# Moving the routing of each head group 13 dots ahead of its first fetch, pacing the linear attention by the fetches, and one more fetch buffer

## The chip, the cores and the metric

The kernel runs on one core of one Trainium2 chip. The metric is the device time in microseconds (us). The kernel before took 2400.81 us, the median of three runs that lie between 2400.66 and 2401.58 us.

## The reference, cut to what matters

256 tokens of width 1024 pass through three blocks: latent attention, gated linear attention and a convolution/attention mixer. The first two are each followed by a PEER layer, the third by a mixture of 32 experts. The change lies in the two PEER layers and in the linear attention between them. A PEER layer picks, for each token and each of 8 heads, 16 rows out of a table of 16384, and sums them with weights that depend on the rows:

```python
def peer_ffn(x, w_query, sub_keys, u_tab, v_tab):        # blocks of 128 tokens
    q = (xi @ w_query).reshape(B, T, 8, 2, 64)
    s = jnp.einsum('bthcd,cnd->bthcn', q, sub_keys)      # 2 x 128 scores per head
    s_top, i_top = lax.top_k(s, 16)
    cand = s_top[..., 0, :, None] + s_top[..., 1, None, :]
    best, pos = lax.top_k(cand.reshape(B, T, 8, 256), 16)
    idx = ...                                            # 16 rows of 16384 per head
    gate = jax.nn.softmax(best, axis=-1)
    h = gelu(jnp.einsum('bthkd,btd->bthk', u_tab[idx], xi))
    return jnp.einsum('bthk,bthkd->btd', gate * h, v_tab[idx])

def gla_mixer(x, ...):                                   # layer 1, between the PEER layers
    proj = x @ w_in                                      # 1024 x 3088
    log_a = log_sigmoid(g_low @ w_g2 + b_g) / 16
    o = chunked_gla(q, k, v, log_a)                      # 4 heads, a state carried over chunks of 64
    return (rms_norm(o) * silu(r)) @ w_o                 # 1024 x 1024
```

Every product is in float32, built from pairs of rounded parts where the code says `mm3`.

## The kernel before, in words

The stages follow each other: latent attention (`mla`), the two PEER layers with the linear attention woven in (`experts`, from some 150 us to 1620 us), the mixer and the mixture of experts. All that changes is in `experts`.

**Dots and fetches.** The tables u and v lie side by side in memory, so that one row has 2048 float32. A *fetch* (`meet`, L849) is an indirect DMA that GpSimd (POOL) issues: 128 tokens each get one row, into one buffer `g` of 128 x 2048. A ring of `NG` = 9 such buffers is used in turn. The *dot* that follows runs on VectorE (DVE, L129): the u half times the token `xs`, summed to `hs`. Two fetches make a pair (`NQ` = 2). After a pair, ScalarE (ACT) takes the Gelu of both sums (L858), DVE multiplies by the gates, ACT builds two diagonal matrices `dw` (L862), and TensorE (PE) adds diag(w) times the v half to the accumulators (L865). Only then is a buffer of the ring free for the fetch 9 further on. There are 2 layers x 2 token blocks x 8 heads x 16 rows = 512 fetches.

**Groups and routing.** The heads are taken in groups of two (in the very first block [0], [1], [2,3], [4,5], [6,7]; later [0,1], [2,3], [4,5], [6,7]). Group starts are therefore at fetch 0, 16, 32, 64, 96, 128 and so on by 32. *Routing* a group (`prepare` = `query`, then `route`) means the query product on PE, the scores, two rounds of top-16 on DVE, the row numbers `idx`, and the gates (`sm`, `gate`, with an exponential on ACT, L831). `prepare` is a Python generator; each `yield` ends one piece. While the dots of one group are written out, the pieces of the next group's routing are taken from the generator between them, `parts` = 7n+4 pieces (n heads) over the first 70% of the dots (`RT`); whatever is left runs after the group's last dot (`for _ in step: pass`). The code behind the last `yield`, which writes `idx` and the gates, runs only when the generator is asked once more than it has yields. It has 7n+4 yields in layer 0, block 0 (each head's query yields twice there), 5n+4 in layer 0, block 1, and 6n+4 in layer 1.

**Linear attention.** `gla` is a generator too, of 84 pieces for block 0 and 80 for block 1. Block 0 runs between the dots of layer 0, block 1 (fetches 128 to 255), block 1 between those of layer 1, block 0 (256 to 383); `BG` = 0.95 pieces per dot are asked for. Its carried state `S` has a tile of its own in the stage's pool.

**Order on the engines.** All DVE instructions of routing and dots are chained in the order in which they are written (`InOrder`); every engine runs its own queue in order, and a scheduler that simulates time decides where instructions of different threads stand in it. Weights come in by DMAs that SyncE (SP) issues, into four `raw` buffers.

Of the kernel before, what the change touches and what calls it, by code (L numbers as in the profile page):

```python
# [9 lines left out]
FT = mybir.dt.float32  # L10
# [109 lines left out]
class InOrder:  # L120

    def __init__(self, tc, engine):
        self.tc, self.engine, self.last = tc, engine, None
# [14 lines left out]
class K:  # L138
    def __init__(self, tc, ins, es):
        self.tc, self.nc, self.i = tc, tc.nc, ins  # L140
        nc = self.nc
        self.cp = es.enter_context(tc.tile_pool(name="cp", bufs=1))
        self.pp = es.enter_context(tc.tile_pool(name="pp", bufs=1))
        cp = self.cp
        self.h = self.pp.tile([128, 2, 1024], FT, name="h", tag="h")
        self.cols = cp.tile([128, NCOLS], FT, name="cols")
        self.iota = cp.tile([128, 128], FT, name="iota")
        nc.gpsimd.iota(self.iota, pattern=[[1, 128]], base=0, channel_multiplier=0,
                       allow_small_or_imprecise_dtypes=True)
        self.diag = cp.tile([128, 128], FT, name="diag")  # L150
        nc.gpsimd.iota(self.diag, pattern=[[1, 128]], base=0, channel_multiplier=-1,
                       allow_small_or_imprecise_dtypes=True)
        self.mhalf = cp.tile([128, 1], FT, name="mhalf")
        nc.gpsimd.memset(self.mhalf, -0.5)
        self.ident = cp.tile([128, 128], FT, name="ident")
        nc.vector.tensor_scalar(self.ident, self.diag, 0.0, None, op0=OP.is_equal)
        self.flip = 0
        self.ssq = {}
        self.psum = es.enter_context(tc.tile_pool(name="banks", bufs=1, space=PSUM, reuse_waits="tile"))
        self.ahead = []  # L160
        self.NQ, self.NG, self.RT, self.BG = 2, 9, 0.7, 0.95
        self.xb = {}
        self.MP, self.G1, self.G2, self.G3, self.G4, self.BK = 34, 0, 4, 2, 1, 3
        self.CP, self.QS, self.KS = 0, 1, 0
        self.gate = None
        self.junk = None
        self.WN, self.W0, self.WL = 5, 12, 4
        self.W1, self.W2 = 20, 13
        self.NRAW, self.NHL, self.NHL1 = 4, 12, 12
# [556 lines left out]
    def experts(self):  # L726
# [3 lines left out]
        with self.phase("peer", ps=(6, 7), pq=(2, 3)) as mp:  # L730
# [15 lines left out]
            def query(l, b, h):  # L746
                if (l, b, h) in qs:
                    return
                if l not in keys:
                    keys[l] = mp.tile([128, 256], FT, name="sk", bufs=2)  # L750
                    nc.sync.dma_start(keys[l], self.i[f"sk{l}"])
                it = its.setdefault((l, b), None) or self.units(self.i[f"pq{l}"])
                its[l, b] = it
                ws = [next(it), next(it)]
                for b in ((0, 1) if l == 0 else (b,)):
                    q = qs[l, b, h] = mp.tile([128, 128], FT, name=f"qT{b}", bufs=8 if b else 3)
                    xH, xL = self.xb[b]
                    p = self.ps("pq")
                    for c in range(8):
                        wH, wL = ws[c // 4]  # L760
                        s = slice((c % 4) * 128, (c % 4 + 1) * 128)
                        self.mm3(p[:, :128], wH[:, s], wL[:, s], xH[:, c, :], xL[:, c, :], c == 0, c == 7)
                    nc.scalar.activation(q, p[:, :128], AF.Copy)  # L763
                    yield
# [74 lines left out]
            def prepare(l, b, hs):  # L839
                for h in hs:  # L840
                    yield from query(l, b, h)
                yield from route(l, b, hs)

            def meet(l, b, idx, gate):
                hs = mp.tile([128, self.NQ], FT, name="hs", bufs=6)
                got = []
                for k in range(self.NQ):
                    g = mp.tile([128, 2, 1024], FT, name="g", bufs=self.NG)
                    nc.gpsimd.indirect_dma_start(out=g.rearrange("p a b -> p (a b)"), out_offset=None,  # L849
                                                 in_=self.i[f"puv{l}"],  # L850
                                                 in_offset=bass.IndirectOffsetOnAxis(ap=idx[:, k:k + 1], axis=0))
                    V.tensor_tensor_reduce(g[:, 0, :], g[:, 0, :], self.xs[b], 1.0, 0.0, op0=OP.mult,
                                           op1=OP.add, accum_out=hs[:, k:k + 1])
                    got.append(g)
                    if k < self.NQ - 1:
                        yield
                w = mp.tile([128, self.NQ], FT, name="w", bufs=6)
                nc.scalar.activation(w, hs, AF.Gelu)  # L858
                V.tensor_tensor(w, w, gate, op=OP.mult)
                for k, g in enumerate(got):  # L860
                    d = mp.tile([128, 128], FT, name="dw", bufs=5)
                    nc.scalar.activation(d, self.ident, AF.Copy, scale=w[:, k:k + 1])  # L862
                    left[l, b] -= 1
                    for n in range(2):
                        mm(y[b][n], d, g[:, 1, n * 512:(n + 1) * 512], start=False, stop=left[l, b] == 0,  # L865
                           skip_group_check=True)
                        if left[l, b] == 0:
                            self.square(b, n, y[b][n])
                yield

            def dots(batches):
                for t in batches:
                    yield from meet(*t)

            groups = []
            for l in range(2):
                for b in range(2):
                    left[l, b] = 128
                    first = [[0], [1]] if l == b == 0 else [[0, 1]]
                    groups += [(l, b, hs) for hs in first + [[2, 3], [4, 5], [6, 7]]]  # L880
            state = mp.tile([128, 4, 2, 256], FT, name="S")
            behind, pace, done = None, 0.0, 0
            for _ in prepare(*groups[0]):
                pass
            for i, (l, b, hs) in enumerate(groups):
                if l != b and hs[0] == 0:
                    behind, pace, done = self.gla(mp, 1 - b, state), 0.0, 0
                step = prepare(*groups[i + 1]) if i + 1 < len(groups) else iter(())
                n2 = len(groups[i + 1][2]) if i + 1 < len(groups) else 0
                parts = 7 * n2 + 4  # L890
                batches, ready = ready, []
                n = int(len(batches) * self.NQ * self.RT)
                taken = 0
                for k, _ in enumerate(dots(batches)):
                    while taken < parts and taken < (k + 1) * parts // n:
                        next(step, None)
                        taken += 1
                    if behind is not None:
                        pace += self.BG
                        while done < pace:  # L900
                            done += 1
                            if next(behind, 0) == 0:
                                behind = None
                                break
                if behind is not None and hs[-1] == 5:
                    for _ in behind:
                        done += 1
                    behind = None
                for _ in step:
                    pass  # L910
            nb = [mp.tile([128, 2, 1024], FT, name="g", bufs=self.NG).rearrange("p a b -> p (a b)")[:, :1024]
                  for _ in range(3)]
            self.load_gain(4, nb[2])
# [336 lines left out]
    def moe(self, out):  # L1250
        nc, tc = self.nc, self.tc
        y = self.y
        with self.phase("moe", ps=(2, 3, 6, 7)) as mp:
# [134 lines left out]
            def experts(once):  # L1388
                wts = weights(once)
                for q in range(8):  # L1390
# [58 lines left out]
                    for b in range(2):  # L1449
                        for n in range(2):  # L1450
                            mm(y[b][n], C[:, b, :], ys[:, n * 512:(n + 1) * 512], start=False, stop=False,
                               skip_group_check=True)

            experts(True)
            fin = self.pp.tile([128, 2, 1024], FT, name="fin", tag="h")
            sq1 = fin[:, 1, 512:640]
# [11 lines left out]
            with tc.For_i(1, rounds, 1):  # L1468
                nc.vector.tensor_scalar(rank, rank, -32.0, None, op0=OP.add)
                experts(False)  # L1470
# [39 lines left out]
```

## Time and profile before

| | before |
|---|---|
| median of the runs | 2400.81 us |
| the profiled execution, its own time | 2398.6 us |
| its span, first to last instruction | 2396.8 us |
| PE busy | 2040.0 us (85%) |
| DVE busy | 1414.2 us (59%) |
| ACT busy | 717.8 us (30%) |
| POOL busy | 618.2 us (26%) |
| mean DMA rate over the span | 355 GB/s |

The busy shares are means over stages with different limits. Within the PEER layers the useful row is the DMA rate in each slice of time: it has a level that it reaches again and again and never passes, and dips below it.

### The profile page before, as it was taken

Reading aid. Unit: us, or ns where it says so; the run is one execution under the profiler, and the core shown is the slowest. Engines: PE = TensorE matmul, PEld = TensorE weight load, DVE = VectorE, ACT = ScalarE, POOL = GpSimd, SP = SyncE. Lnnn points to the kernel's source line nnn. Section 1 sums busy time; section 2 is a strip of 40 time slices with the busy share of each in tenths; the row PEclk is TensorE's granted clock in tenths of the full one; section 3 lists DMA queues with packets and bytes.
Section 4 is the critical chain, followed back from the end, with each engine's and each line's share of the span. In section 5 each row is a group of like instructions: output and inputs, shape, how many; then the busy total and the mean of one; then the engine's idle time right before and its main releaser. Section 6 shows DMA issues by size and latency. Waiting matters only on the chain. (4 is left out here: it accounts for less than half of the span.)

```text
span 2396.8 us, 26752 instructions
## 1 busy us (share of the span) xinstructions
PE 2040.0 (85%) x8294; PEld 1078.1 (45%) x8296; DVE 1414.2 (59%) x3813; ACT 717.8 (30%) x1756; POOL 618.2 (26%) x665
## 2 busy tenths in 40 slices
PE   8998667678989778998887777779999989999997
PEld 7774223234445325654333332237899942222221
DVE  7767667668868667878766776657666640000001
ACT  6632211235343225544222221215545510000000
POOL 4123433443434442333444444320000000000000
PEclk9999999998999998999999999999999999999999
DMA  4369889999999998999999999984467699999996
GB/s 154 106 227 371 343 368 422 373 422 408 421 388 360 421 421 352 422 401 399 422 421 421 421 421 422 421 335 150 150 226 260 221 360 417 417 417 417 417 417 277
DMA packets 161780, 851.40 MB, mean 355 GB/s; under 512 B 18368, under 2 KB 19008, under 8 KB 96096
## 3 DMA queue, kind: packets, MB, share of 16 engines
q0 software_dynamic: 73728, 536.90, 54.4%
q1 hardware_dynamic: 87616, 312.20, 33.6%
q8 instruction: 69, 1.13, 0.2%
q14 instruction: 79, 0.65, 0.1%
q10 hardware_dynamic: 288, 0.52, 0.1%
HBM read 848.50 MB, written 1.05 MB: 354 GB/s over the span
## 5 line engine op out<-in xcount | busy, mean ns | idle before, releaser
L865 PE MATMUL ps<-g,dw 128*128 128x512 f32 x2048 | 973.8, 622 | 253.2 <-ACT dw L862 252.2
L849 POOL DMA_INDIRECT g<-in_puv_dram,idx x512 | 558.4, 1091 | 882.1 <-PE ps L865 482.6
L129 DVE CUSTOM_DVE_ANT_0 g<-g,xs 128x1024 f32<-128x1024 f32 x512 | 623.1, 1221 | 232.5 <-DMA g<-in_puv_dram,idx 221.3
L865 PEld LDWEIGHTS ps<-g,dw 128*128 128x128 f32 x2048 | 386.7, 197 | 787.8 <-issue 388.3
L262 DVE TENSOR_TENSOR wl<-raw,wh 128x512 fp32r<-128x512 f32 (+3 forms) x404 | 267.9, 678 | 118.9 <-ACT wh L260 107.7
L260 ACT ACTIVATE wh<-raw 128x512 fp32r<-128x512 f32 (+3 forms) x408 | 242.3, 614 | 150.8 <-PE ps L285 124.4
L858 ACT ACTIVATE w<-hs 128x2 f32<-128x2 f32 x256 | 51.9, 203 | 745.6 <-DVE hs L129 745.5
L1425 PE MATMUL ps<-we,xT 128*32 128x512 f32 x788 | 186.2, 600 | 21.2 <-DMA we<-in_e_gu_dram 21.2
L862 ACT ACTIVATE dw<-ident,w 128x128 f32<-128x128 f32 x512 | 177.4, 393 | 70.6 <-DVE w L129 66.4
L1430 DVE TENSOR_TENSOR hid<-hid,ps 128x512 f32<-128x512 f32 x8 | 5.5, 688 | 248.9 <-PE ps L1425 248.9
L284 PE MATMUL ps<-xH,wh 128*128 128x256 f32 (+1 forms) x456 | 130.3, 286 | 1.1 <-DVE sel L1117 1.1
L286 PE MATMUL ps<-xL,wh 128*128 128x256 f32 (+1 forms) x456 | 130.3, 286 | 0.0
L285 PE MATMUL ps<-xH,wl 128*128 128x256 f32 (+1 forms) x456 | 129.9, 285 | 0.0
L1425 PEld LDWEIGHTS ps<-we,xT 128*32 128x32 f32 x788 | 35.6, 108 | 162.9 <-DMA we<-in_e_gu_dram 119.0
L1459 POOL MEMSET fin<- 128x128 f32 x1 | 0.2, 204 | 405.5 <-PE ps L1425 405.5
L1443 PE MATMUL ps<-we,hT 128*32 128x512 f32 x400 | 96.4, 597 | 0.1
L284 PEld LDWEIGHTS ps<-xH,wh 128*128 128x128 f32 (+1 forms) x456 | 87.0, 191 | 2.9 <-issue 1.5
L286 PEld LDWEIGHTS ps<-xL,wh 128*128 128x128 f32 (+1 forms) x456 | 87.0, 191 | 1.1 <-issue 1.1
L285 PEld LDWEIGHTS ps<-xH,wl 128*128 128x128 f32 (+1 forms) x456 | 87.0, 191 | 0.7 <-issue 0.6
L129 DVE TENSOR_TENSOR w<-w,gate 128x2 f32<-128x2 f32 x256 | 41.2, 161 | 75.7 <-ACT w L858 75.7
L284 PE MATMUL ps<-x,wh 128*128 128x128 f32 (+1 forms) x272 | 78.8, 293 | 3.1 <-ACT qT L763 2.4
L286 PE MATMUL ps<-x,wh 128*128 128x128 f32 (+1 forms) x272 | 74.7, 278 | 0.0
(443 smaller groups left out, 2480.9 us busy)
## 6 DMA issues: line engine op xcount, KB each, us to landing
we<-in_e_gu_dram SPq DMA_DIRECT2D x197, 512.0 KB
we<-in_e_dn_dram SPq DMA_DIRECT2D x100, 512.0 KB
raw<-in_gla_w_dram SPq DMA_DIRECT2D x48, 512.0 KB
wx<-in_e_gu_dram SPq DMA_DIRECT2D x35, 512.0 KB
raw<-in_pq_dram SPq DMA_DIRECT2D x24, 512.0 KB
raw<-in_mx_conv_dram SPq DMA_DIRECT2D x24, 512.0 KB
raw<-in_e_gu_dram SPq DMA_DIRECT2D x24, 512.0 KB
g<-in_puv_dram,idx POOLq DMA_INDIRECT x512
```

What stands on the lines that cost most here:

```text
L129: r = f(*a, **k)
L260: nc.scalar.activation(H[:, :n], src, AF.Copy)
L262: e.tensor_tensor(L[:, :n], src, H[:, :n].bitcast(FT), op=OP.subtract)
L284: mm(out, aH, bH, start=start, stop=False, **kw)
L285: mm(out, aL, bH, start=False, stop=False, **kw)
L286: mm(out, aH, bL, start=False, stop=stop, **kw)
L849: nc.gpsimd.indirect_dma_start(out=g.rearrange("p a b -> p (a b)"), out_offset=None, in_=self.i[f"puv{l}"], in_offset=bass.IndirectOffsetO ...
L858: nc.scalar.activation(w, hs, AF.Gelu)
L862: nc.scalar.activation(d, self.ident, AF.Copy, scale=w[:, k:k + 1])
L865: mm(y[b][n], d, g[:, 1, n * 512:(n + 1) * 512], start=False, stop=left[l, b] == 0, skip_group_check=True)
L1425: mm(p[e * 32:(e + 1) * 32, :], xg[:, c, e * 32:(e + 1) * 32], ws[e][:, u * 512:(u + 1) * 512], start=c == 0, stop=c == 7, skip_group_chec ...
L1443: mm(pd[n][e * 32:(e + 1) * 32, :], hT[:, c, e * 32:(e + 1) * 32], ws[e][:, n * 512:(n + 1) * 512], start=c == 0, stop=c == 3, skip_group_ ...
```

## The change

The diff does four things.

1. A `plan` fixes for each group the dot at which its routing begins and the dot at which it has to be complete: `ends` = the group's first fetch minus `LEAD` (13), or 4 dots per group at the very start. The pieces are spread evenly from the end of the previous group's routing to that dot; at that dot the rest is run, including the code behind the last `yield`. The first group of a block in layer 1 begins `LATE` = 36 dots before its first fetch, since the tokens must have passed the linear attention.
2. `parts` is now 6n+4, and n more where the layer number equals the block number.
3. The linear attention is asked for 1.0 pieces per dot; it is completed at the latest 36 dots before the next block's first fetch.
4. The ring has 10 fetch buffers. The state `S` moves out of the stage's pool into the place of the residual tile `h`, which nobody reads in these stages; both the state and one fetch buffer take 8 KB per partition.

```diff
-        self.NQ, self.NG, self.RT, self.BG = 2, 9, 0.7, 0.95
+        self.NQ, self.NG, self.LEAD, self.LATE, self.BG = 2, 10, 13, 36, 1.0
...
-            state = mp.tile([128, 4, 2, 256], FT, name="S")
-            behind, pace, done = None, 0.0, 0
+            state = self.pp.tile([128, 2, 1024], FT, name="S", tag="h").rearrange("p a (b c) -> p (a b) c", c=256)
+            state = state.rearrange("p (h c) d -> p h c d", c=2)
+
+            starts = np.concatenate([[0], np.cumsum([16 * len(hs) for _, _, hs in groups])])
+            ends = [max(int(t) - self.LEAD, 4 * j) for j, t in enumerate(starts)]
+            plan = []
+            for j in range(1, len(groups)):
+                l, b, hs = groups[j]
+                begin = ends[j - 1] if l == 0 or hs[0] else int(starts[j]) - self.LATE
+                parts = 6 * len(hs) + 4 + len(hs) * (l == b)
+                plan.append((begin, ends[j], parts, groups[j]))
...
-                n = int(len(batches) * self.NQ * self.RT)
-                taken = 0
-                for k, _ in enumerate(dots(batches)):
-                    while taken < parts and taken < (k + 1) * parts // n:
-                        next(step, None)
-                        taken += 1
+                for _ in dots(batches):
+                    slot += 1
...
-                for _ in step:
-                    pass
+                    while plan and slot >= plan[0][0]:
+                        begin, end, parts, group = plan[0]
+                        if step is None:
+                            step, due = prepare(*group), 0
+                        n = (slot - begin) * parts // max(1, end - begin)
+                        while due < n and slot < end:
+                            next(step, None)
+                            due += 1
+                        if slot < end:
+                            break
+                        for _ in step:
+                            pass
+                        plan.pop(0)
+                        step = None
```

What this does to the engines' queues is seen in three places.

VectorE, the end of the routing of heads [4,5] of the first block, whose first fetch is number 64 (`ISA g,hs` and `ISA hs` are one dot, `w` the pair's weights; `idx_2799` and `gate_2803` are the new group's row numbers and gates). Before:

```order
L129 ISA g_2782,hs_2781<-g_2782,xs_1471 128x1024
L129 ISA hs_2781 128x1
L129 ISA g_2785,hs_2781<-g_2785,xs_1471 128x1024
L129 ISA hs_2781 128x1
L129 TENSOR_TENSOR w_2788<-w_2788,gate_2304 128x2
L129 SCALAR_TENSOR_TENSOR row_2676<-row_2676,red_2675 128x32
L129 CAST idx_2799<-row_2676 128x32
L129 TENSOR_TENSOR gate_2803<-best_2644 128x32
L129 TENSOR_REDUCE sm_2802<-gate_2803 128x2
L129 RECIPROCAL sm_2802<-sm_2802 128x2
L129 TENSOR_TENSOR gate_2803<-gate_2803,sm_2802 128x32
L129 ISA g_2810,hs_2809<-g_2810,xs_1471 128x1024
```

The same instructions now (`idx_2677`, `gate_2681`):

```order
L129 SCALAR_TENSOR_TENSOR row_2640<-row_2640,red_2639 128x32
L129 CAST idx_2677<-row_2640 128x32
L129 TENSOR_TENSOR gate_2681<-best_2590 128x32
L129 TENSOR_REDUCE sm_2680<-gate_2681 128x2
L129 RECIPROCAL sm_2680<-sm_2680 128x2
L129 TENSOR_TENSOR gate_2681<-gate_2681,sm_2680 128x32
L129 ISA g_2687,hs_2669<-g_2687,xs_1471 128x1024
L129 ISA hs_2669 128x1
L129 TENSOR_TENSOR w_2690<-w_2690,gate_2182 128x2
L129 ISA g_2702,hs_2701<-g_2702,xs_1471 128x1024
L129 ISA hs_2701 128x1
L129 ISA g_2742,hs_2701<-g_2742,xs_1471 128x1024
```

Before, 64 dots stand in the queue ahead of the new row numbers, and the next dot is already one of the new group. Now 51 stand ahead of them, and the following pair is still weighted with the old group's gate (`gate_2182`). For all groups the number of dots ahead of `idx` was 0, 16, 32, 64, 96, 115, 147, 179, 211, 245 and so on by 32 up to 469; now it is 0, 4, 19, 51, 83, 113, 145, 177, 209, 243, 275, 307, 339, 370, 402, 434, 466.

ScalarE, the start of the second linear attention (`e`, `eb`, `en`, `ed` are its gates; `wh` copies of weights; `sc` scores of a routing; `w`, `dw` belong to pairs of dots). Before, the end of what stands between the pair 258/259 and the pair 260/261:

```order
L774 ACTIVATE sc_6196<-ps_6194 128x256
L774 ACTIVATE sc_6287<-ps_6285 128x256
L260 ACTIVATE wh_6293<-raw_6291 128x512
L1084 ACT_TABLE_LOAD
L1084 ACTIVATE e_6168<-e_6168 128x512
L260 ACTIVATE wh_6317<-raw_6291 128x512
L1085 ACT_TABLE_LOAD
L1085 ACTIVATE e_6168<-e_6168 128x512
L260 ACTIVATE wh_6332<-raw_6330 128x512
L260 ACTIVATE wh_6353<-raw_6330 128x512
L858 ACT_TABLE_LOAD
L858 ACTIVATE w_6223<-hs_6205 128x2
```

Now, between the pair 266/267 and the pair after it:

```order
L1094 ACT_TABLE_LOAD
L1094 ACTIVATE e_6190<-e_6190 128x512
L862 ACTIVATE dw_6369<-ident_69,w_6366 128x128
L862 ACTIVATE dw_6373<-ident_69,w_6366 128x128
L1095 ACT_TABLE_LOAD
L1095 ACTIVATE e_6190<-e_6190 128x512
L969 ACT_TABLE_LOAD
L969 ACTIVATE eb_6251<-bc_6229 128x512
L970 ACTIVATE en_6252<-bc_6229 128x512
L971 ACTIVATE ed_6253<-z_6189 128x512
L858 ACT_TABLE_LOAD
L858 ACTIVATE w_6405<-hs_6384 128x2
```

Scores and weight copies no longer stand in that stretch, and it comes some eight dots later. On TensorE 98 matmuls of queries and linear attention stood between two pairs at dot 260 before, the most anywhere in the PEER layers; now the most is 61, at dot 312.

GpSimd, the fetches and what stands between them (`st`, `gst` are powers for norms, `att` a clearing), at the first linear attention, old rows with a minus, new ones with a plus:

```order
-L849 DMA g<-in_puv_dram,idx 128x2048 x137
+L849 DMA g<-in_puv_dram,idx 128x2048 x138
 L317 TENSOR_TENSOR st<-st,mhalf 128x1
-L849 DMA g<-in_puv_dram,idx 128x2048 x23
-L1001 MEMSET att 128x512
-L849 DMA g<-in_puv_dram,idx 128x2048 x22
+L849 DMA g<-in_puv_dram,idx 128x2048 x26
+L1011 MEMSET att 128x512
+L849 DMA g<-in_puv_dram,idx 128x2048 x24
 L292 TENSOR_TENSOR gst<-gst,mhalf 128x1
-L849 DMA g<-in_puv_dram,idx 128x2048 x7
+L849 DMA g<-in_puv_dram,idx 128x2048 x10
```

The first power of a head stood behind 182 fetches and now stands behind 188; VectorE makes its input after 175 dots before and after 180 now, so that 7 and now 8 fetches are between the two.

## Rows read from the trace of the kernel before

**Rows 1.** Page, DMA rate in 40 slices of 59.9 us
```profile
GB/s 154 106 227 371 343 368 422 373 422 408 421 388 360 421 421 352 422 401 399 422 421 421 421 421 422 421 335 150 150 226 260 221 360 417 417 417 417 417 417 277
```
**Rows 2.** Page, DMA queue of the fetches: packets, MB, share
```profile
q0 software_dynamic: 73728, 536.90, 54.4%
```
**Rows 3.** Stretches: PE, PEld, DVE, ACT, POOL busy, granted clock, DMA share, GB/s
```profile
190.00:210.00 20.00, 15.38 (x45) 7.32 (x44) 8.83 (x23) 5.72 (x13) 6.30 (x7) 0.97 0.67 269
240.00:260.00 20.00, 12.35 (x24) 5.15 (x24) 12.29 (x30) 5.49 (x12) 6.25 (x6) 0.83 0.51 190
330.00:350.00 20.00, 9.94 (x22) 3.63 (x20) 7.92 (x19) 4.59 (x9) 7.98 (x8) 0.88 0.67 259
420.00:430.00 10.00, 7.40 (x16) 2.88 (x16) 3.98 (x14) 4.59 (x9) 2.64 (x3) 1.00 0.39 136
1280.00:1600.00 320.00, 243.13 (x532) 97.81 (x533) 212.16 (x548) 67.95 (x208) 130.14 (x127) 0.97 1.01 421
```
**Rows 4.** Timeline of POOL, fetches 64 and 65: start, length, idle before
```profile
339.88 0.94 POOL L849 DMA_INDIRECT g<-in_puv_dram,idx  x1 [15.84 <-issue]
341.13 0.94 POOL L849 DMA_INDIRECT g<-in_puv_dram,idx  x1 [0.30 <-issue]
```
**Rows 5.** Timeline of DVE at the same group's start
```profile
338.64 0.16 DVE L129 TENSOR_TENSOR w<-w,gate 128x2 f32<-128x2 f32 x1 [0.27 <-ACT w L858]
338.94 0.18 DVE L129 CAST idx<-row 128x32 int32<-128x32 f32 x1
```
**Rows 6.** Timeline of DVE and POOL around the first routing and first dots
```profile
138.37 0.29 DVE L129 MAX8 top<-sc 128x8 f32<-128x128 f32 x1
152.61 1.23 POOL L849 DMA_INDIRECT g<-in_puv_dram,idx  x1 [20.44 <-DVE gate L129]
158.56 1.22 DVE L129 CUSTOM_DVE_ANT_0 g<-g,xs 128x1024 f32<-128x1024 f32 x1 [2.05 <-DMA g<-in_puv_dram,idx]
165.71 0.16 DVE L129 TENSOR_TENSOR w<-w,gate 128x2 f32<-128x2 f32 x1 [0.82 <-ACT w L858]
```
**Rows 7.** Stretches, columns as in Rows 3, of both linear attentions
```profile
500.00:1280.00 780.00, 660.87 (x2023) 339.40 (x2021) 585.52 (x1529) 289.24 (x707) 301.34 (x272) 0.96 0.99 404
560.00:570.00 10.00, 10.00 (x23) 4.86 (x22) 9.73 (x27) 4.24 (x11) 5.00 (x4) 0.81 0.91 338
700.00:730.00 30.00, 29.68 (x97) 16.56 (x96) 21.43 (x46) 12.73 (x37) 10.73 (x10) 1.00 0.84 319
740.00:770.00 30.00, 28.53 (x99) 17.10 (x100) 25.73 (x85) 9.12 (x27) 11.54 (x9) 0.83 0.92 342
930.00:960.00 30.00, 24.65 (x69) 14.39 (x69) 25.46 (x64) 18.41 (x34) 8.21 (x7) 0.85 0.77 286
1050.00:1070.00 20.00, 18.56 (x60) 9.77 (x59) 18.10 (x53) 10.31 (x30) 9.20 (x9) 1.00 0.95 358
1100.00:1130.00 30.00, 29.37 (x126) 18.07 (x124) 20.54 (x40) 11.85 (x32) 10.10 (x9) 0.95 0.99 386
```
**Rows 8.** Timeline of ACT at the second linear attention's start
```profile
904.84 0.20 ACT L858 ACTIVATE w<-hs 128x2 f32<-128x2 f32 x1
926.71 1.28 ACT L858 ACT_TABLE_LOAD   x1
928.00 0.20 ACT L858 ACTIVATE w<-hs 128x2 f32<-128x2 f32 x1
```
**Rows 9.** Timeline of POOL behind it
```profile
933.49 1.52 POOL L849 DMA_INDIRECT g<-in_puv_dram,idx  x1 [22.13 <-PE ps L865]
```
**Rows 10.** Timeline of PE, two pairs, and the stretch of the second
```profile
1487.78 3.70 PE L865 MATMUL ps<-g,dw 128*128 128x512 f32 x8 [1.28 <-ACT dw L862]
746.19 6.28 PE L865 MATMUL ps<-g,dw 128*128 128x512 f32 x8
740.00:750.00 10.00, 8.53 (x26) 5.89 (x27) 9.86 (x23) 3.46 (x9) 0.00 (x0) 0.56 1.00 408
```

More of the change, by code (lines that the diff above doesn't have):

```diff
@@ L880, in experts @@
                     groups += [(l, b, hs) for hs in first + [[2, 3], [4, 5], [6, 7]]]
-            state = mp.tile([128, 4, 2, 256], FT, name="S")
-            behind, pace, done = None, 0.0, 0
+            state = self.pp.tile([128, 2, 1024], FT, name="S", tag="h").rearrange("p a (b c) -> p (a b) c", c=256)
[8 more added lines that the diff above has]
+                plan.append((begin, ends[j], parts, groups[j]))
             for _ in prepare(*groups[0]):
                 pass
-            for i, (l, b, hs) in enumerate(groups):
+            behind, step, due, slot = None, None, 0, 0
+            for j, (l, b, hs) in enumerate(groups):
                 if l != b and hs[0] == 0:
[L887 to L890, printed above, removed]
+                    behind, until, done, pace = self.gla(mp, 1 - b, state), slot + 128 - self.LATE, 0, 0.0
                 batches, ready = ready, []
-                n = int(len(batches) * self.NQ * self.RT)
-                taken = 0
-                for k, _ in enumerate(dots(batches)):
-                    while taken < parts and taken < (k + 1) * parts // n:
-                        next(step, None)
-                        taken += 1
+                for _ in dots(batches):
+                    slot += 1
                     if behind is not None:
                         pace += self.BG
-                        while done < pace:
+                        while behind is not None and (done < pace or slot >= until):
                             done += 1
@@ L903, in experts @@
                                 behind = None
[L904 to L908, printed above, removed]
-                for _ in step:
-                    pass
+                    while plan and slot >= plan[0][0]:
[12 more added lines that the diff above has]
+                        step = None
             nb = [mp.tile([128, 2, 1024], FT, name="g", bufs=self.NG).rearrange("p a b -> p (a b)")[:, :1024]
```

## The prediction

> **What bounds the kernel now.** I read the DMA rate by slices first [rows 1]. From slice 4 to slice 26, the PEER layers, the rate comes back to 421 or 422 GB/s again and again and never passes it, while the busy shares of the engines move; so in these stages the transfers are the limit and every dip below that level is lost time. A long quiet stretch confirms it: from 1280 to 1600 us the DMA engines are busy throughout at 421 GB/s while PE is busy 243 of 320 us and DVE 212 [rows 3]. One fetch is 536.90 MB / 512 = 1.049 MB [rows 2], or 2.49 us at that rate. A dip is worth (421 - its rate) / 421 times its length.
>
> Four dips lie in the first block, at 190 to 210, 240 to 260, 330 to 350 and 420 to 430 us [rows 3]. They are worth 7.2, 11.0, 7.7 and 6.8 us, together 32.7 us. The third is shown closely: POOL issues nothing for 15.84 us and then starts fetch 64 at 339.88 us, 0.9 us after DVE has written the group's row numbers at 338.94, which it does only behind the last pair's weights at 338.64 [rows 4, 5]. The trace calls the wait "issue", but the next fetch follows at 0.30 us distance, so buffers were free: what was missing was the row numbers. The reason is in the count of pieces: in layer 0, block 0 the generator has exactly as many yields as it is asked for, so the code behind the last one runs after the group's last dot. That holds for the groups at fetch 16, 32, 64 and 96 and for no other.
>
> A second set of dips belongs to the two linear attentions, in six stretches between 560 and 1130 us [rows 7]. They are worth 2.0, 7.3, 5.6, 9.6, 3.0 and 2.5 us, together 30.0 us. Here POOL waits for PE to free a buffer: up to 22.13 us before the fetch at 933.49 [rows 9]. Behind that, ACT takes the Gelu of one pair at 904.84 and of the next at 928.00 [rows 8], because in its queue, and in PE's and DVE's, a block of queries, weight copies and gates of the linear attention stands between the two.
>
> **The change, part by part.**
>
> *Row numbers 13 dots early.* The four dips of the first block lose their cause. Fetch 64 now needs `idx` behind dot 51 and a buffer that dot 54 frees (ring of 10), so the buffer decides, by three dots or 7.5 us. In the other groups the numbers stood 10 to 13 dots ahead already and cost nothing. I take all 32.7 us. The instructions are the same in number, and no byte of transfer is added or removed. The gates now come in the middle of a group: DVE waits there for ACT's exponential, about two table loads of 1.28 us [rows 8], with dots queued behind the wait, and the ring's ten fetches, 24.9 us of transfers, cover it.
>
> *The squeeze at the start.* What is late next: head 1 has to be routed within the first four dots. The routing of one head, from its first maximum to the fetch that it releases, took 152.61 - 138.37 = 14.2 us [rows 6], with some weight work mixed in. It now stands behind the first pair's weights at 165.71 and in front of dot 4, which so comes at 165.7 + 14.2 + two dots of 1.3 (1.22 [rows 6] and reading the sum) = 182.5 us. Two dots more and ACT's way back to Gelu (1.28) bring its pair's weights to some 187, and PE, at 3.70 us for a pair [rows 10], frees its buffer at 189. By then 14 fetches have been issued (10 buffers and the four of dots 0 to 3), 34.9 us of transfers that began at about 155 (first issue 152.61, first dot 158.56 [rows 6]) and last until 190. It is just covered. The term lies between nothing and the whole 14.2 us; I take 2 us, since the sum of rows ends within a microsecond of the cover.
>
> ACT changes its table on the way, from Gelu to the exponential and back; a load takes 1.28 us in the trace [rows 8], and the next instruction starts when it ends. [...]
>
> *One more buffer.* Where transfers are always queued it gives nothing. In each of the six dips of rows 7 it covers one more fetch, 2.49 us, but no more than the dip holds: 2.0 + 4 x 2.49 + 2.49 = 14.5 us.
>
> *The spreading.* The worst cluster of before, 98 matmuls between two pairs at dot 260, is gone: the routing of [2,3] in layer 1 begins at dot 243 instead of 256, ahead of the linear attention instead of on top of it. That was the 9.6 us dip, so 7.1 us beyond the buffer's share. The heads' state updates around dot 186 to 200, behind the dips from 700 to 770, are drawn apart by some five dots, which may give more. Against it: the linear attention's chain of four table loads with its exponentials and the scan between them now stands in one piece at dot 268, and there are groups of 61 and 52 matmuls at dots 312 and 338. No row shows these. The gates chain lay between two pairs 23 us apart in before together with a block of queries [rows 8], so alone it is below the ring's 24.9 us. The term for buffer and spreading together has the ends 30.0 us gained (all dips gone) and 10 us lost (a new dip like the worst). I take 20 us, that is 14.5 + 7.1 less 1.6 for what new clusters cost; of the rows the nearest is the quiet stretch, where evenly spread work left no dip at all [rows 3].
>
> POOL's powers stand 8 fetches behind their inputs in a ring of 10 instead of 7 in a ring of 9, so this wait, too, leaves one fetch more in flight. The move of `S` costs nothing: the residual tile was read last before the PEER layers, and the next one is written after them. SP's weight loads have the same number and the same four buffers; they move with the pieces that use them.
>
> *The sum*, on the profiled execution's own 2398.6 us: -32.7 + 2 - 20 = -50.7, or 2347.9 us. The median of the runs is 2.2 us above that execution, which gives 2350 us. The stages behind the PEER layers keep their instructions and start so much earlier.
>
> **The rivals.**
>
> *Only the first block gains.* The linear attention's dips are moved, not filled, and what the tenth buffer covers is lost to the new clusters. For it: the chain at dot 268 and the 61 matmuls; DVE is busy 586 of 780 us there and PE 661 [rows 7], so little is left to catch up with. Against it: the six dips are each below 10 us, and the clusters get smaller. Time: 2398.6 - 32.7 + 2 + 2.2 = 2370 us.
>
> *The dip moves to the front.* The row numbers are early, but the squeeze costs its full 14.2 us, since DVE is 14 us behind with everything from dot 4 on and the ring runs empty. For it: the cover is within a microsecond. Against it: DVE has 1.3 us of work per dot against 2.49 us of transfer, so it catches up until dot 9, when the next routing begins. Time: 2350 + 12 = 2362 us.
>
> [...]
>
> [...]
>
> *That the change does not do what it says* I hold for excluded: the order of the built program shows the row numbers 13 dots ahead in these groups.
>
> **How the numbers follow.** The forecast of 2350 us has a chance of 0.70, the first rival (2370) 0.17, the second (2362) 0.07, the clock 0.03, and 0.03 is left for something not thought of. If every dip went, the time would be 2398.6 - 62.7 + 2.2 = 2338 us; that and the runs' spread set the lower end, 2336. The upper end, 2380, takes in the first rival with a new dip of 10 us. A measurement of this kernel can tell 0.2%, 4.8 us, from no change. The forecast and the first two rivals are faster by far more, 0.94 together; of the 0.03 left a third goes to each side: 0.95 faster, 0.01 the same, and 0.04 slower with the clock.
>
> **What would show it.** In the profile after, fetches 16, 32, 64 and 96 follow the one before within some 5 us, and the rate is 421 GB/s through the first block from some 190 us on. A pause before fetch 14 measures the squeeze. In the linear attentions (by then some 30 us earlier) the sum of dips should be near 10 us instead of 30; near 30 is the first rival. [...] The prediction is wrong if the rate holds at its level and the time still does not fall, or if a later stage takes the gain back.

## The result, and the profile after

The changed kernel takes 2363.91 us (median of four runs, 2359.84 to 2367.02) against 2401.19 us of the kernel before on the same chip (2400.66 to 2401.96): a ratio of 0.9843, 95% interval 0.9826 to 0.9861, or 37.3 us less. The forecast was 2350 us, 50.7 us less. The profiled execution of the changed kernel is the slowest of its four runs, 2367.0 us with a span of 2365.2 us; it stands 31.6 us below the profiled one of before. Its account by stages, bounded by the starts of dots 128, 256 and 384 on DVE:

| us | up to dot 128 | dots 128 to 256 | 256 to 384 | the rest | span |
|---|---|---|---|---|---|
| before | 514.4 | 380.3 | 396.7 | 1105.5 | 2396.8 |
| after | 490.4 | 377.0 | 390.2 | 1107.6 | 2365.2 |
| difference | -24.0 | -3.3 | -6.5 | +2.1 | -31.6 |
| forecast | -30.7 | -20 for both | | 0 | -50.7 |

The DMA rate by slices of the page after, below the clock of the same slices, answers to [rows 1]:

```profile
PEclk9999999999999998999899999999999999999999
GB/s 156 99 213 384 418 421 421 421 420 422 422 385 375 409 421 418 394 421 421 371 421 421 421 421 421 422 262 171 143 242 259 223 380 417 417 418 417 418 417 275
```

From slice 5 to slice 11 the rate now stays at its level, where before it fell to 343, 368 and 373. The dips that are left stand in slice 4, at the start of the first block, and in slices 12 to 20, the two linear attentions.

Stretches of the changed kernel in its first block, columns as in [rows 3]: the two dips that are left (the prediction's sum had none but the 2 us of the squeeze), and two stretches that were dips before.

```profile
190.00:200.00 10.00, 10.00 (x26) 4.69 (x26) 9.07 (x28) 2.57 (x9) 4.77 (x5) 1.00 0.91 343
230.00:240.00 10.00, 10.00 (x25) 4.39 (x24) 7.76 (x18) 2.69 (x9) 7.04 (x6) 0.98 0.75 266
330.00:350.00 20.00, 15.35 (x36) 6.17 (x35) 13.53 (x39) 3.97 (x13) 7.49 (x8) 1.00 1.01 421
420.00:430.00 10.00, 6.45 (x15) 2.50 (x14) 6.57 (x30) 1.79 (x6) 4.27 (x4) 1.00 1.01 419
```

The stretches 330 to 350 and 420 to 430, with 259 and 136 GB/s before, are full. POOL around fetch 64 and DVE's row numbers for it, in the changed kernel, answer to [rows 4, 5]:

```profile
311.40 0.94 POOL L849 DMA_INDIRECT g<-in_puv_dram,idx  x1 [0.30 <-issue]
312.84 0.94 POOL L849 DMA_INDIRECT g<-in_puv_dram,idx  x1 [0.50 <-DVE hs L129]
```
```profile
298.59 0.38 DVE L129 CAST idx<-row 128x32 int32<-128x32 f32 x1
```

Fetch 64 (312.84) follows the one before by 1.44 us, and its row numbers have been ready for 14 us; before, it waited 15.84 us for them. The two linear attentions, answering to [rows 7]: both whole blocks (490 to 867 and 867 to 1258) and the dips in them.

```profile
490.00:867.00 377.00, 322.78 (x916) 159.31 (x916) 288.94 (x750) 134.39 (x338) 150.17 (x136) 0.95 1.00 407
690.00:720.00 30.00, 27.48 (x83) 14.51 (x82) 20.68 (x64) 10.02 (x32) 11.41 (x10) 0.92 0.86 316
730.00:790.00 60.00, 55.72 (x209) 32.42 (x208) 45.36 (x95) 21.75 (x60) 28.16 (x24) 0.97 0.98 382
867.00:1258.00 391.00, 347.39 (x1117) 187.51 (x1118) 295.91 (x770) 145.75 (x364) 156.71 (x136) 0.94 0.99 409
940.00:980.00 40.00, 37.43 (x135) 21.74 (x134) 26.79 (x68) 13.13 (x36) 13.07 (x14) 0.91 0.97 375
1120.00:1130.00 10.00, 9.64 (x24) 4.11 (x23) 9.25 (x20) 1.80 (x6) 6.42 (x5) 1.00 0.94 355
1150.00:1160.00 10.00, 10.00 (x24) 4.71 (x23) 4.20 (x10) 3.29 (x9) 2.87 (x3) 0.73 0.51 189
```

By the two whole-block rows the loss is (421 - 407) / 421 x 377 = 12.5 and (421 - 409) / 421 x 391 = 11.1 us, 23.7 together. The prediction set 10 as the mark of its forecast and 30 as that of "only the first block gains"; this is nearer to the second. By the same measure both together lost (421 - 404) / 421 x 780 = 31.5 us before [rows 7]. The granted clock is 0.95 and 0.94, where both together had 0.96 before [rows 7].

### The profile page after: what moved, and what is told of

Same layout as the page of the kernel before. It is cut to its first block, busy times and chain, and to the rows that moved or that the text cites. A ratio compares the mean times of both kernels' runs of the same rounds, so it can differ in the third digit from the quotient of the medians.

```text
span 2365.2 us, 26677 instructions
## 1 busy us (share of the span) xinstructions
PE 2049.9 (87%) x8294; PEld 1085.0 (46%) x8296; DVE 1417.0 (60%) x3813; ACT 708.8 (30%) x1751; POOL 625.1 (26%) x665
## 5 line engine op out<-in xcount | busy, mean ns | idle before, releaser
L129 DVE TENSOR_TENSOR w<-w,gate 128x2 f32<-128x2 f32 x256 | 41.3, 161 | 80.7 <-ACT w L858 80.6
L284 PE MATMUL ps<-x,wh 128*128 128x128 f32 (+1 forms) x272 | 81.3, 301 | 2.2 <-ACT qT L763 2.2
L286 PE MATMUL ps<-x,wh 128*128 128x128 f32 (+1 forms) x272 | 77.4, 287 | 1.8 <-issue 1.4
```

The source lines that it names most:

```text
L129: r = f(*a, **k)
L284: mm(out, aH, bH, start=start, stop=False, **kw)
L286: mm(out, aH, bL, start=False, stop=stop, **kw)
```

## The experiments

Each ratio is to the kernel before on the same chip; the first four, the next four and the last four kernels ran on three chips, on which the kernel before took 2396 to 2397 us. The stage columns come from one profile each, as above. Where nothing before or in a stage differs, they still move: e6, e8, e9 and e11 have the program of the change up to dot 128, in the same order on every engine, and reach that dot after 486.1 to 489.9 us, the change after 490.4.

| kernel | us | ratio (95%) | to dot 128 | 128-256 | 256-384 |
|---|---|---|---|---|---|
| e1_idx | 2370.4 | 0.9887 (0.9872-0.9902) | 488.1 | 380.1 | 394.2 |
| e2_routing | 2361.2 | 0.9855 (0.9840-0.9871) | 490.0 | 376.9 | 385.2 |
| e3_ring10 | 2384.0 | 0.9944 (0.9930-0.9957) | 512.4 | 369.5 | 391.5 |
| e4_ring9 | 2365.9 | 0.9875 (0.9860-0.9890) | 488.2 | 376.0 | 393.9 |
| e5_idx_ring10 | 2361.6 | 0.9850 (0.9836-0.9864) | 486.2 | 374.1 | 393.8 |
| e6_pace095 | 2355.0 | 0.9838 (0.9821-0.9855) | 486.1 | 376.2 | 385.3 |
| e7_soft_start | 2357.8 | 0.9833 (0.9819-0.9846) | 487.6 | 377.4 | 386.9 |
| e8_warm | 2362.3 | 0.9849 (0.9834-0.9864) | 486.1 | 383.2 | 384.9 |
| e9_again | 2361.6 | 0.9850 (0.9836-0.9863) | 489.9 | 377.4 | 389.9 |
| e10_both | 2357.9 | 0.9838 (0.9824-0.9851) | 489.2 | 374.6 | 385.0 |
| e11_heads | 2369.8 | 0.9887 (0.9872-0.9902) | 486.9 | 375.8 | 394.8 |
| e12_both_heads | 2358.4 | 0.9833 (0.9817-0.9848) | 488.2 | 377.8 | 384.7 |

**The change taken apart.**

e1_idx, from the kernel before:

```diff
-                parts = 7 * n2 + 4
+                parts = 7 * n2 + 5
```

> The kernel before with one number changed: one more piece is asked for in each group, so the code behind the generator's last yield (the row numbers) runs at 70% of the group's dots, not behind its last. Ring of 9, linear attention and order otherwise as before. Theory A (the row numbers are what the change gives, the rest gives little): the dips at fetches 16, 32, 64 and 96 go, 32.7 us in the rows of before, with perhaps 2 to 4 left where the lead is only 5 dots (fetches 16 and 32): 2368 to 2373 us, so as far as the whole change within some 7 us. Rival B (buffer and spreading give about 20 us as forecast, and the row numbers less than was read from the dips, because something else is late next): 2382 to 2390 us.

26.1 us by the medians, 27.1 by the ratio, of the change's 37 are in this one number; both linear attentions stay as before within 2.5 us. Theory A holds. The dip that is left (fetch 32 still comes 10.6 us after the one before), and one that is filled:

```profile
230.00:250.00 20.00, 12.69 (x26) 5.38 (x25) 17.04 (x41) 6.70 (x17) 6.68 (x6) 0.83 0.88 348
330.00:350.00 20.00, 14.91 (x33) 5.75 (x32) 12.72 (x32) 3.59 (x12) 7.50 (x8) 1.00 1.01 421
```

e2_routing, from the changed kernel (and `S` back in its old pool; the block's last dot for the linear attention is put at 96 instead of 92, which decides nothing, since its 84 pieces end at dot 88):

```diff
-        self.NQ, self.NG, self.LEAD, self.LATE, self.BG = 2, 10, 13, 36, 1.0
+        self.NQ, self.NG, self.LEAD, self.LATE, self.BG = 2, 9, 13, 36, 0.95
```

> The changed kernel's plan for the routing (13 dots ahead, first two groups within 4 and 8 dots) with the ring of 9 and with the linear attention paced as before (0.95 pieces per dot, rest flushed at the end of the third group). Theory A: the four dips go (32.7), the squeeze at the start takes back about 7 (the dips at 190 to 200 and 230 to 240 us in the changed kernel's trace): 2372 to 2378 us. Rival B: 2380 us or more, since buffer and spreading have to make up the 37 us of the whole change. A third way: the linear attention with the routing ahead of it is better placed already, 2366 to 2370.

2361.2 us, below even the band of the third way: with the ring of 9 the plan is as fast as the whole change, if the pace stays at 0.95. It is 9.2 us faster than e1 on the same chip, and the intervals of the two do not meet. By the stages the second linear attention gains most of that, 385.2 us against 394.2.

e3_ring10, from the kernel before (with `S` moved as in the change):

```diff
-        self.NQ, self.NG, self.RT, self.BG = 2, 9, 0.7, 0.95
+        self.NQ, self.NG, self.RT, self.BG = 2, 10, 0.7, 0.95
```

> The kernel before with a ring of 10 buffers (S moved to the residual tile's pool as in the change), nothing else. Theory A: in the first block's dips a tenth buffer can give nothing, since the fetch waits for numbers that stand behind the dot of the last fetch issued; in the linear attentions' six dips it gives about 6 of the 30 us: 2393 to 2398 us. Rival B (forecast): 14.5 us, 2384 to 2389. Third: nothing at all, 2400 to 2402.

13.4 us: rival B's size, the forecast's 14.5. Theory A is wrong on the size and right on the place; the first block gains 2.0 us, the linear attentions 10.8 and 5.2. Its two blocks in stretches:

```profile
512.00:882.00 370.00, 313.48 (x867) 153.07 (x868) 285.67 (x755) 129.98 (x330) 152.36 (x135) 0.96 1.01 416
882.00:1273.00 391.00, 339.56 (x1150) 183.44 (x1148) 297.88 (x770) 153.29 (x372) 153.28 (x135) 0.97 1.00 411
```

The loss is 4.4 and 9.3 us, 13.7 together, 10 less than in the changed kernel, though its ring is no longer.

e4_ring9, from the changed kernel: `NG` 9 instead of 10, nothing else.

> The changed kernel with the ring of 9 instead of 10. Theory A: loses some 3 to 8 us: 2367 to 2372 us. Rival B (the tenth buffer gives 14.5): 2376 to 2380.

A microsecond below theory A's band: without its tenth buffer the change has 30.0 us instead of 37, so the buffer is worth 6 to 8 in it (against 0.9843, and 0.9850 in e9). The intervals just touch, and the stage columns do not show it: up to dot 384 they add to 1258.1 us here, 1257.6 in the change and 1257.2 in e9. Against e2 on the same chip it is 4.7 us slower, with intervals that overlap; the two differ by the pace (and by where `S` lies). The second linear attention takes 393.9 us instead of 385.2.

**Do the parts add up?**

e5_idx_ring10 is e1 and e3 together, without the plan and with the pace of before.

> The first and the third experiment together: the kernel before with the row numbers at 70% of the group and a ring of 10; its routing windows and its pacing of the linear attention stay. Theory C (row numbers about 26 us and tenth buffer 13 us add up, and the change's new places for the routing and the linear attention take part of it back): the dips left are 4.4 in the first block and some 5 and 10 in the two linear attentions, about 46 us below before: 2350 to 2356 us, faster than the whole change. Rival D (the tenth buffer's gain depends on the late row numbers and is gone once these are early): 2361 to 2367, as the whole change.

The median lies in rival D's band and no run reaches theory C's: 0.985, as the whole change, 36.0 us below before, where 27.1 and 13.4 would give 40.5. But the 4.5 us between are no more than the three intervals allow together, so that the two gains do not add is likely and not shown. Beside the early row numbers the tenth buffer gives some 9 us (0.985 / 0.9887), by the stages 6.0 in the first linear attention and nothing in the second. As this kernel has neither the plan nor the new pace, these two together give nothing on top of the tenth buffer; that the plan gives something without it is in e2.

e6_pace095, from the changed kernel: `BG` 0.95 instead of 1.0 (and 96 for 92, as above).

> The changed kernel with the linear attention paced as before, 0.95 pieces per dot (1.0 in the change), the rest flushed at dot 96 instead of 92 of its block; that is the second experiment with a ring of 10. Theory C, with the pace as what takes the gain back (2361.2 against 2365.9 us at ring 9): 2354 to 2359 us. If it is the routing's windows instead: 2361 to 2365, as the change. If 0.95 was an accident of the ring of 9: 2363 to 2368.

2355.0 us, in theory C's band; the second linear attention takes 385.3 us instead of 390.2. The interval still holds the change's 0.9843 and 0.9850.

e7_soft_start, from the changed kernel:

```diff
-            ends = [max(int(t) - self.LEAD, 4 * j) for j, t in enumerate(starts)]
+            ends = [max(int(t) - self.LEAD, 8 * j) for j, t in enumerate(starts)]
```

> The changed kernel with head 1 routed within eight dots instead of four (8 j instead of 4 j), so its row numbers are 8 dots ahead of fetch 16. Theory C: the dips of the changed kernel at 160 to 200 us (2.5 us) go, dot 4 starts 5 to 8 us earlier, and the one at 230 to 240 (3.7 us), which comes from the exponential of the gates standing in ACT's queue, stays: 2 to 3 us faster than the change, 2360 to 2363. If the squeeze is behind that one as well: 2357 to 2359. If the pieces only land elsewhere: 2364 to 2367.

Dot 4 starts at 172.7 us instead of 185.5, and at 172.7 to 173.6 also in e10 and e12, which have the same edit: the squeeze is eased. Dot 128 comes 2.8 us earlier, no earlier than in e6, e8 and e11, which do not have the edit. The dip from 220 to 240 us shrinks from 3.8 us to 1.5 (389 GB/s), and the time is in the band of the second expectation, that the squeeze is behind this dip too. The other runs speak against it: with the squeeze eased the dip is 4.1 us in e10 and 4.3 in e12, and without it 1.3 in e6 and 1.1 in e8. The ratio, 0.9833, is 0.0010 and 0.0017 below those of the change, within their intervals.

**The dip of the clock.**

e8_warm, from the changed kernel:

```diff
-        self.norm_b(b, self.xs[b])
+        self.norm_b(b, self.xs[b], warm=10)
```

> The changed kernel with ten matmuls on a tile that nobody reads, placed on PE where the linear attention's last part waits for the normed rows (PE idle 2.79 us in the changed kernel's trace before the clock falls and 48 query matmuls run at 0.21 us instead of 0.11). Clock theory: the granted clock stays up, the pair behind takes 3.7 instead of 6.3 us, and the dip at 1150 us (5.5 us) shrinks to 1 or 2: 2358 to 2361 us. Rival (the dip is the in-order chain's, whatever the clock): 2363 to 2367, with the dummies' own time on top.

Stretches of the changed kernel at that place, then PE there (start, length, idle before it):

```profile
1136.00:1140.00 4.00, 1.20 (x8) 0.53 (x7) 2.40 (x6) 1.25 (x4) 1.80 (x2) 1.00 1.01 416
1140.00:1144.00 4.00, 3.13 (x16) 2.60 (x17) 3.86 (x13) 3.95 (x6) 0.00 (x0) 0.72 1.02 427
1144.00:1148.00 4.00, 4.00 (x21) 4.00 (x20) 3.60 (x8) 1.40 (x5) 0.00 (x0) 0.50 1.02 422
1148.00:1152.00 4.00, 4.00 (x14) 2.97 (x14) 3.59 (x7) 1.68 (x6) 0.00 (x0) 0.50 0.70 289
1152.00:1156.00 4.00, 4.00 (x8) 1.66 (x6) 2.16 (x6) 1.01 (x3) 0.99 (x1) 0.58 0.15 28
```
```profile
1139.27 1.31 PE L1080 MATMUL ps<-ident,xs 128*128 128x128 f32 x8 [2.79 <-DVE xs L320]
...
1150.07 6.29 PE L865 MATMUL ps<-g,dw 128*128 128x512 f32 x8
```

The same place with the ten matmuls, and the whole of its dip:

```profile
1142.00:1146.00 4.00, 4.00 (x38) 4.00 (x38) 3.38 (x9) 3.39 (x7) 0.00 (x0) 1.00 1.00 419
1146.00:1150.00 4.00, 4.00 (x13) 2.04 (x13) 3.73 (x8) 1.76 (x6) 1.31 (x1) 1.00 1.02 420
1150.00:1154.00 4.00, 4.00 (x12) 2.04 (x11) 3.08 (x8) 1.59 (x6) 2.58 (x3) 1.00 0.89 320
1150.00:1160.00 10.00, 10.00 (x27) 4.69 (x26) 7.98 (x16) 4.04 (x11) 7.36 (x7) 1.00 0.94 350
```
```profile
1136.80 2.32 PE L331 MATMUL ps<-junk,iota 128*128 128x512 bf16 x10 [0.78 <-ACT junk L299]
1138.95 1.18 PE L1080 MATMUL ps<-ident,xs 128*128 128x128 f32 x8
...
1146.53 3.60 PE L865 MATMUL ps<-g,dw 128*128 128x512 f32 x8
```

PE was busy 1.20 of 4 us, and from 1144 to 1152 us the clock then stood at 0.50; the pair behind took 6.29 us. With the gap filled the clock stays at 1.00, the pair takes 3.60, and the dip costs 1.7 us instead of 5.5. So the clock theory is shown for this dip. The stage takes 384.9 us, 5.3 less than in the change and 2.0 less than in e7 on the same chip; beyond this dip the change lost 3.8 us at 960 to 980, which are not lost here, and no row ties that to the ten matmuls. The time as a whole, 2362.3 us, is in neither band and unchanged (0.9849): the same ten matmuls also stand at the end of the first linear attention, and that stage takes 383.2 us instead of 377.0 and, in e7, 377.4. Why it loses there is open.

**The last four.**

> The changed kernel once more, unchanged, to stand beside the next three on one chip and to give a second profile of it. Expected 2360 to 2365 us. The first block's program is the same as in the sixth and eighth experiments, whose profiles show dips of 2.1 us there and dot 4 some 7 us later than before, against 6.7 and 14.1 in the first profile of the change: if that difference is chance from run to run, this one may show either; if it belongs to the chip, it shows the smaller.

2361.6 us, and the stages of the first profile within 0.5 us; dot 4 is 12.9 us later than before. So the profile repeats on another chip. Dot 4 comes only some 7 us later in e6 and e8, whose program is the same up to there. The profile of the change shows where most of the difference lies, in a copy of weights on ACT and what DVE makes of it:

```profile
167.78 0.63 ACT L260 ACTIVATE wh<-raw 128x512 fp32r<-128x512 f32 x1 [5.38 <-remote]
```
```profile
168.44 0.69 DVE L262 TENSOR_TENSOR wl<-raw,wh 128x512 fp32r<-128x512 f32 x1 [4.29 <-ACT wh L260]
```

In e9 the same copy waits 3.96 us, in e6 and e8 it starts at 161.0 and 160.8 us without this wait. "Remote" means that the profile names no instruction as the releaser; `raw` is where weights land, so a weight load that comes late behind the first fetches is likely, and not shown.

e10_both has the edits of e6 and e7.

> Eight dots for head 1 (seventh experiment) and pace 0.95 (sixth) together. If both gains are real and apart: 2352 to 2356 us, some 6 us under the change on the same chip. If each was within the runs' spread: 2358 to 2363, as the change.

2357.9 us, 3.8 below e9 on the same chip with intervals that overlap. That lies between the two expectations and is no better than e6 or e7 alone: no sum of gains is shown.

e11_heads, from the changed kernel (with pace 1.1):

```diff
-            if b == 0:
-                yield 1
+            yield 1
...
+            yield 1
             st = new("gst", 2, bufs=4)
...
+            yield 1
             nc.vector.scalar_tensor_tensor(r[:, hv], p[:, :256], st[:, 1:2], ...)
```

> The changed kernel with each head of the linear attention cut into three pieces instead of one or two (matmuls of the state, matmuls and squares of the output, normalisation), so that a pair of the experts' rows stands between the steps of its chain; pace 1.1, so that the linear attention ends at the same dot, 84 of its block. Theory E (the dips at 690 to 720 us, 8.2 us of the 13.6 in that block, are the chain PE to DVE to PE to ACT to DVE to POOL to DVE that stands in one piece in every engine's queue): these dips fall to 2 to 4 us, 2357 to 2360 us. Rival F (PE or ACT have simply too much to do there, however it is cut): dips as before, 2361 to 2366; with 1.1 pieces per dot in the projections the dips there may grow by 2 or 3.

Theory E falls: in the median it is 8 us slower than e9, above both bands (its profiled execution, 2364.2 us, is the fastest of its four). The dip at 690 to 720 us shrinks only from 7.5 to 5.1 us, and a new one opens in the second linear attention, here in stretches:

```profile
950.00:960.00 10.00, 8.46 (x50) 8.27 (x49) 4.50 (x10) 2.78 (x6) 0.00 (x0) 0.67 1.00 412
960.00:970.00 10.00, 7.55 (x16) 4.46 (x17) 5.15 (x15) 2.01 (x7) 0.00 (x0) 0.67 0.08 32
970.00:980.00 10.00, 10.00 (x27) 5.22 (x26) 9.80 (x25) 6.19 (x15) 6.34 (x5) 0.94 0.70 266
```

It costs 9.2 + 3.7 = 12.9 us, with the clock at 0.67. In e12, with the same cut and a pace of 1.04, the loss there is 2.6 us, and the dip at 690 to 720 is back at 7.9. So the cut alone does not fill that dip; whether it or the pace of 1.1 opens the new one stays open.

> The tenth and eleventh together (head 1 in eight dots, heads cut in three, pace 1.04 so that the linear attention ends at dot 88 to 89). If all gains are real: 2348 to 2353 us. If only one of the two: 2354 to 2358. If none: as the change.

2358.4 us, at the edge of "only one of the two". No version beats the change beyond its interval: e6, e7, e10 and e12 have ratios 0.0005 to 0.0017 lower, 1 to 4 us.

## Why the prediction was right and wrong

Direction and range were right, and the reading of the bound with them: time lost is DMA rate lost, below a level of 421 to 422 GB/s in the slices of both pages. Of 50.7 us forecast the profile shows 31.6 and the medians 37.3. By the prediction's steps:

*Row numbers 13 dots early* (-32.7): right in the cause, a little large in the size. The four dips are gone, and e1 finds 26 to 27 us for the same cause with a lead of 10 dots, and of only 5 at fetches 16 and 32, where it keeps a dip.

*The squeeze* (+2): the profile has dot 4 at 185.5 us (182.5 forecast) and fetch 14 at 192.13 (189), and it cost 2.4 us between 160 and 200. That the times fit so well is in part luck: 4.29 us of them are DVE's wait for the weight copy (see e9), of which the working knew nothing, and in e6 and e8, without this wait, dot 4 comes at 178.8 and 178.5 us and the loss is 0.5. What was missing is a second dip, behind the routing of heads [2,3]: of the gates in the middle of a group the prediction said that the ring's ten fetches cover them, and here they did not. ACT in the changed kernel:

```profile
215.00 0.20 ACT L858 ACTIVATE w<-hs 128x2 f32<-128x2 f32 x1 [1.64 <-DVE hs L129]
...
223.33 0.23 ACT L831 ACTIVATE gate<-gate 128x32 f32<-128x32 f32 x1 [5.90 <-DVE gate L129]
223.58 1.28 ACT L858 ACT_TABLE_LOAD   x1
225.40 0.20 ACT L858 ACTIVATE w<-hs 128x2 f32<-128x2 f32 x1 [0.54 <-DVE hs L129]
```

The exponential stands in ACT's queue ahead of the next pair's Gelu and waits 5.90 us for DVE, which has the row-number code and a dot in front. The pair's weights come 10.4 us after the last, and the dip from 220 to 240 costs 3.8 us. This wait stands in every run that has the plan, 5.90 us in e6 too, where the dip costs 1.3. So the wait is shown and the size of the dip is not explained; it lies between 1.1 and 4.3 us in the ten kernels with the plan. The table load takes 1.28 us, and the Gelu behind it then waits 0.54 us for DVE.

*Buffer and spreading* (-20): the step that failed. It measured 9.8 us by the stages, and 9 to 11 by the ratios of the change (0.9843, and 0.9850 in e9) to e1 (0.9887). The buffer's share (14.5) was a sound reading of the kernel before: e3 measured 13.4. But it was added to a kernel that has other edits beside it: 9 us are left beside the early row numbers (e5), 6 to 8 in the change (e4). The steps from 13 to 9 and on to 6 to 8 are each within the intervals; both point the same way. The spreading's share (7.1 - 1.6) is there when the buffer is not: e2 is 9 us faster than e1, most of it in the second linear attention, where the prediction looked for it. On top of the buffer it does not show: e5, without it, is as fast as the change; its first linear attention is 2.9 us shorter than the change's, the second 3.6 longer. The new pace, which the prediction gave no price of its own, may have taken part of it back: with 1.0 instead of 0.95 the second linear attention takes 393.9 us instead of 385.2 with nine buffers (e4, e2) and 390.2 instead of 385.3 with ten (the change, e6). Against that, e7 has 386.9 at a pace of 1.0, and the intervals of each of these two pairs of runs overlap. So the two terms together measured about half of the forecast; how the missing half is divided is not shown.

One place where the changed kernel loses more than e3 is the heads of the linear attention, dots 180 to 192. With ten buffers DVE needs 41.3 us for these twelve dots in e3, 43.8 and 43.9 in e10 and e6, 44.2 in e5, 47.1 in the change and 47.2 in e9. The dips there (690 to 720 us; in e3, whose dots come some 23 us later, 730 to 740) cost 0.9 us, then 4.9 and 6.1, 4.8, 7.5 and 8.5. That looks like a stretch which the ring covers up to some length, but e4 does not fit: with nine buffers it needs 46.8 us and loses 1.1.

```profile
690.00:720.00 30.00, 26.50 (x82) 15.53 (x81) 24.69 (x65) 12.35 (x33) 10.03 (x9) 0.91 1.00 406
```

Nor is the pace all of it: with nine buffers and 0.95 (e2) the dots take 47.5 us. What sets the size of this dip stays open. Two engines of the changed kernel there, ACT and PE, and two stretches:

```profile
684.40 0.38 ACT L1048 ACTIVATE junk<-ps 128x256 f32<-128x256 f32 x1 [7.43 <-PE ps L1044]
...
698.85 0.39 ACT L1048 ACTIVATE junk<-ps 128x256 f32<-128x256 f32 x1 [7.46 <-PE ps L1044]
```
```profile
675.93 0.70 PE L1029 MATMUL ps<-v,kdt 64*128 64x256 f32 x2 [2.72 <-ACT r L1023]
676.55 5.40 PE L865 MATMUL ps<-g,dw 128*128 128x512 f32 x8
...
687.56 1.06 PE L1029 MATMUL ps<-v,kdt 64*128 64x256 f32 x2 [2.24 <-DVE r L1050]
...
690.75 5.59 PE L865 MATMUL ps<-g,dw 128*128 128x512 f32 x8
```
```profile
676.00:682.00 6.00, 6.00 (x11) 2.37 (x12) 2.80 (x7) 0.97 (x3) 0.95 (x1) 0.72 1.01 414
690.00:694.00 4.00, 4.00 (x6) 1.52 (x5) 2.40 (x10) 0.47 (x2) 1.46 (x1) 0.50 0.94 387
```

PE idles 2.72 and 2.24 us for one step of a head's chain, and the pair of dots that follows takes 5.40 and 5.59 us instead of 3.70 [rows 10], at a granted clock of 0.72 and 0.50; ACT waits 7.43 and 7.46 us for the head's matmuls behind it, and the next pair's Gelu waits behind ACT. Such slow pairs stand in spots and not over the whole stage, whose granted clock is 0.95. That the clock is the cause here too was not tried; e8 shows it for the dip at 1150 us. Why the same code runs these dots 2.9 us slower in e5 than in e3 stays open; the two differ by one piece more that each group is asked for.

*The rivals.* "Only the first block gains" (2370 us) saw the linear attentions better than the forecast did: 23.7 us of dips are left, where it said 30. "The dip moves to the front" (2362 us) hit the time, but for another reason, since the front took back 6 us and not 14: that is luck. Of the clock, which has 0.03 among the chances of the prediction, no run shows a slower kernel: the granted clock is 0.94 to 0.98 in both linear attentions of all fourteen profiles. The rest, from dot 384 on, kept its time within 2.1 us.

## What to carry to other kernels

Before a dip is filled with a longer buffer ring, look at what is late at its bottom: where the fetch waits for its address, as here at the four group starts, earlier addresses helped (26 to 27 of 37 us came from one number), and a tenth buffer alone did not (in e3 the rate from 330 to 350 us is 256 GB/s, 259 before). Measure the gain of a cover on the kernel that already has the other edits before adding it to theirs: the tenth buffer gave 13 us alone, 9 beside the early row numbers and 6 to 8 in the whole change. Give each number that a change sets its own experiment, the pace as well: here the plan at the old pace with nine buffers was as fast as everything together. And before a dip's size is explained by one edit, look at it in the other runs that share the edit: the one at 230 us shrank in one of three.

## What the runs showed of the hardware

After a stretch in which PE was busy 1.20 of 4 us, the granted clock stood at 0.50 from 1144 to 1152 us although PE was then busy 8 of 8 us; ten matmuls on a tile that nobody reads, 2.32 us long, kept it at 1.00. From 1152 to 1156 us it stood at 0.58, with PE busy throughout. The same program does not take the same time in one place each time: up to dot 128, the change and the four kernels with its program there took 486.1 to 490.4 us, and a copy of weights that waited 5.38 us in one profile waited not at all for the same in another.
